# A decoder step on one core: new durations for the clocks that place small products, a search over priorities in the list scheduler, and a shorter patience in two passes

## The chip, the core and the metric

The kernel runs on one core of a Trainium2 chip. A core has five engines that each work through their own instructions in order: TensorE (PE in the profile, with its weight loads as PEld), VectorE (DVE), ScalarE (ACT), GpSimd (POOL) and SyncE (SP), which mostly issues DMA transfers. The metric is the device time of one execution in microseconds; the median of the runs counts.

## The reference

One layer of a hybrid decoder for 1024 prompt rows and 8 x 8 sample rows (1088 columns in all, features on the partitions): a normalised and modulated input, one projection to 34 blocks of 128 columns, a recurrent branch, a pooling branch, a gated merge, and an MLP.

```python
h = rms_norm(x, lp["norm_mix"]) * (1 + sc) + sh
P = h @ lp["w_in"]
pr, pp, pg = jnp.split(P, [RWKV_COLS, RWKV_COLS + POOL_WIDTH], axis=-1)
o_r, s_shift, s_wkv, v_first = rwkv7_branch(pr, shift0[l], wkv0[l], v_first, lp)
o_p, s_pool = pool_branch(pp, pool0[l], pos0, lp)
g_r, g_p = jnp.split(jax.nn.sigmoid(pg), 2, axis=-1)
merged = g_r * (o_r @ lp["w_br_rwkv"]) + g_p * (o_p @ lp["w_br_pool"])
x = x + gt * (merged @ lp["w_out"])
...
x = x + gt * (jnp.square(jax.nn.relu(h @ lp["w_ff1"])) @ lp["w_ff2"])

def step(S, inp):                                   # the recurrence, per head of 64
    r_t, w_t, k_t, v_t, kk_t, a_t = inp
    sa = jnp.einsum("bhvk,bhk->bhv", S, -kk_t)
    S = (S * w_t[:, :, None, :] + sa[..., None] * (kk_t * a_t)[:, :, None, :]
         + v_t[..., None] * k_t[:, :, None, :])
    return S, jnp.einsum("bhvk,bhk->bhv", S, r_t)
```

## The kernel before, in words

**Two kinds of products.** The large matrices run as *weight products*: a 128x128 piece of a weight, split by ScalarE into a rounded half `whi` and by VectorE into the rest `wlo` (read from `wraw`), times up to 364 columns of the split input (`hx`). They go into the PSUM banks `mm` (four) and are evicted to `px`, `d` or `t`. The recurrence runs beside them as *small products* in four *passes* f = 0 to 3 of two heads each, in the banks `w` (two) and `wc` (two). The recurrence is done in 16 chunks of 64 rows with a matrix inverse for each, and then a *chain* over the chunks.

**A pass, by the names in the profile.** `front` and `unit` make decays and scores (`w<-ra,bk`, `w<-kct,ra`, `w<-kct,bk`, `w<-uv,at`); `bonus` and `post` make sums over a head with a matrix of ones (`w<-wt,bones`). `inverse` runs on VectorE: fifteen pairs of a multiply and a reduction (`hv`, `tt`), then transposes (`iv`). `level` completes it with four groups of 32x32 products: `w<-hv,hv`, `w<-iv,hv`, `w<-hv,ao`, `w<-z,hv`. `affine` follows with `w<-at,z` and `wc<-ab,at` or `w<-ab,at`. `chain` takes the products `wc<-uv,ab` and `wc<-ab,uv`, then 16 steps in which the small products `wc<-S,ra` and `wc<-ra,S` use the state S that VectorE made in the step before. `sample` does the eight short sequences (`w<-uv,ak`, `w<-hv,ra` and others). `post(f - 1)` normalises and gates the output of the pass before (`w<-wt,sw` is its gate; in `post(3)` the sums are `w<-wt,kct`) and writes it to scratch in HBM (`d_or`); pass 0 has modulation products in that place (`wc<-wt,sT`, "ada"). The last weight products of this stage are the eight `op_job`s, whose evictions `px<-px,mm` and `d<-d,mm` are on VectorE; the next stage starts with `or_job(0)`, which needs the output of `post(3)` in its fourth quarter.

**What sets the order.** Python generators emit the kernel. `Pace.run` emits weight products one after the other and asks, between them, whether a small product may go: it may when `Clocks` holds its operands ready (`Need.at`, with a spare of 300 ns) at the present time of the emitted stream. If the last product was a full 128x128 one, the small one waits up to `wait` ns more for another that changes the shape of the array (its *patience*). Each instruction on another engine gets a duration in `Clocks.op` and a place on its engine in `Clocks.place`; each small product gets one in `K.took`. So these durations set the order on PE.

The same instructions are recorded in `Ledger`, with a second set of durations in `Ledger.cost` and `Ledger.product`. After the stage is emitted, `Ledger.schedule` *plays* it: a list scheduler in which PE keeps its order and the other engines take, of the instructions that are ready, the one with the least key. The key was the place in which it was emitted. `Ledger.fix` then pins the order of VectorE, and of SP from its 61st issue, to that of the play; ScalarE and GpSimd are not pinned.

## Time and profile before

| | |
|---|---|
| median of 3 runs | 1584.08 us (1583.99 to 1584.94) |
| the profiled execution | 1583.99 us |
| its span, first to last instruction | 1582.2 us |
| mean granted clock of TensorE | 0.994 |
| PE, PEld, DVE, ACT, POOL busy | 96%, 91%, 70%, 42%, 9% of the span |
| instructions | 34017 |

The stage with the small products lies from about 62 us (the first stage's end) to about 735 us. How to read the rows: a line is "engine line operation output<-inputs, shape, count", then the busy time, the mean duration, and the idle time just before with the one that ended it. In a timeline a row starts with its start and its length in us, and the bracket at its end is the engine's idle time before it, with what ended it. A row of the waits has the total, the number of waits and the longest. Nearly everything on VectorE and ScalarE has one line of the code, that of the recording helper, so the names of the tiles tell the groups apart. A plain fp32 product is recorded twice, which is why its counts are double those of the program.

### The profile page before, as it was taken

To read this page: it belongs to the slowest core of one execution; us is meant where nothing else is said; L and a number is where in the kernel's file an instruction comes from. 1 tells how busy PE (TensorE), PEld (TensorE's weight loads), DVE (VectorE), ACT (ScalarE), POOL (GpSimd) and SP (SyncE) were. 2 spreads that over 40 slices of the span, in tenths; PEclk is the share of its full clock that TensorE was granted. 3 is DMA by queue.
4 is the path that set the end of the run, shared out by engine and by line. 5 is a ranking of instruction groups with operands and counts; after the bars stand their busy time and mean duration, and the time that the engine had idled before them with its cause. 6 is when DMAs were issued, how large, how long until landed. Compare 5 with 4: busy or idle time off the path is not lost.

```text
span 1582.2 us, 34017 instructions
## 1 busy us (share of the span) xinstructions
PE 1526.2 (96%) x13777; PEld 1432.5 (91%) x13777; DVE 1111.3 (70%) x1944; ACT 658.5 (42%) x1285; POOL 147.9 (9%) x234
## 2 busy tenths in 40 slices
PE   4999999999999999999999999999999999999997
PEld 2998888898898899888899999999999999999997
DVE  5576668776777758556544797898767796666776
ACT  5454354355236433423222572222334344334652
POOL 3100100000000000112501210000000050000000
PEclk9999999999999999999999999999999999999999
DMA  9142523244324344854875555665436995664754
GB/s 367 63 136 83 182 86 110 93 133 149 111 78 150 116 125 139 305 188 169 310 280 181 185 196 186 221 219 191 146 146 223 396 348 199 211 208 148 231 164 159
DMA packets 136493, 290.04 MB, mean 183 GB/s; under 512 B 36976, under 2 KB 41072, under 8 KB 136336
## 3 DMA queue, kind: packets, MB, share of 16 engines
q1 hardware_dynamic: 129952, 266.75, 49.2%
q10 hardware_dynamic: 4320, 14.00, 2.6%
q0 software_dynamic: 2064, 7.13, 1.4%
q8 instruction: 108, 1.77, 0.5%
q14 instruction: 49, 0.40, 0.1%
HBM read 210.54 MB, written 77.28 MB: 182 GB/s over the span
## 4 chain that ended last, share of the span: by engine, by line
PE 48%; DVE 11%; DMA 7%; issue 2%; ACT 1%; SPq 0%; POOL 0%; DVEq 0%; ACTq 0%; POOLq 0%
PE mm L573 32%; PE wc L573 8%; PE w L573 7%; DVE hx L393 4%; DMA hid<-in_w_ff 2%; DVE wt L393 2%; DMA d_t<-hx 1%; DVE wlo L393 1%; DMA mg<-in_w_ff 1%; DMA wt<-d_bv 1%; DMA hid<-in_w_ada_mlp 1%; DVE hid L393 1%; DVE mg L393 1%; DVE sw L393 0%; DMA wraw<-in_w_br 0%
## 5 line engine op out<-in xcount | busy, mean ns | idle before, releaser
L573 PE MATMUL mm<-hx,whi 128*128 128x362 f32 (+2 forms) x2944 | 687.5, 321 | 8.4 <-DVE hx L393 2.4
L573 PEld LDWEIGHTS mm<-hx,whi 128*128 128x128 f32 x2944 | 494.7, 189 | 31.0 <-issue 9.4
L573 PE MATMUL mm<-hx,wlo 128*128 128x362 f32 (+2 forms) x1472 | 461.9, 314 | 1.2 <-DVE wlo L393 1.1
L573 PEld LDWEIGHTS mm<-hx,wlo 128*128 128x128 f32 x1472 | 278.1, 189 | 2.0 <-DVE wlo L393 2.0
L573 PE MATMUL mm<-mg,whi 128*128 128x272 f32 (+2 forms) x1312 | 249.0, 289 | 1.3 <-DVE t L393 0.8
L573 PEld LDWEIGHTS mm<-mg,whi 128*128 128x128 f32 x1312 | 205.3, 188 | 6.7 <-issue 2.7
L573 PE MATMUL mm<-mg,wlo 128*128 128x272 f32 (+2 forms) x656 | 188.5, 287 | 0.0
L573 PE MATMUL wc<-hx,whi 128*128 128x272 f32 x896 | 170.4, 287 | 0.0
L393 ACT ACTIVATE whi<-hid 128x512 fp32r<-128x512 f32 x128 | 80.4, 630 | 144.3 <-PE mm L573 53.3
L573 PEld LDWEIGHTS wc<-hx,whi 128*128 128x128 f32 x896 | 140.3, 188 | 0.0
L573 PE MATMUL wc<-hx,wlo 128*128 128x272 f32 x448 | 128.9, 288 | 0.7 <-DVE wlo L393 0.7
L573 PEld LDWEIGHTS mm<-mg,wlo 128*128 128x128 f32 x656 | 123.5, 188 | 0.0
L393 DVE TENSOR_TENSOR wlo<-hid,whi 128x512 fp32r<-128x512 f32 x128 | 88.0, 690 | 40.1 <-ACT whi L393 39.0
L393 DVE TENSOR_TENSOR wlo<-wraw,whi 128x512 fp32r<-128x512 f32 x82 | 58.3, 711 | 62.8 <-ACT whi L393 62.7
L573 PE MATMUL w<-hx,whi 128*128 128x272 f32 (+1 forms) x480 | 97.4, 296 | 1.6 <-ACT hx L393 1.5
L393 ACT ACTIVATE whi<-wraw 128x512 fp32r<-128x512 f32 x100 | 62.6, 627 | 67.2 <-PE mm L573 26.2
L393 POOL TENSOR_TENSOR hx<-hx,rs 128x64 f32<-128x64 f32 x24 | 36.8, 1532 | 568.9 <-DMA mg<-in_w_ff 374.9
L573 PEld LDWEIGHTS wc<-hx,wlo 128*128 128x128 f32 x448 | 84.2, 188 | 1.1 <-DVE wlo L393 1.1
L573 PEld LDWEIGHTS w<-hx,whi 128*128 128x128 f32 x480 | 77.0, 188 | 3.0 <-ACT hx L393 1.8
L573 PEld LDWEIGHTS mm<-mg,hx 128*128 128x128 f32 x576 | 72.8, 188 | 5.0 <-issue 5.0
L573 PE MATMUL mm<-mg,hx 128*128 128x272 f32 (+2 forms) x576 | 74.7, 289 | 0.0
L393 ACT ACTIVATE px<-mm 128x362 f32<-128x362 f32 (+3 forms) x113 | 46.4, 435 | 60.6 <-PE mm L573 57.3
(293 smaller groups left out, 2317.0 us busy)
## 6 DMA issues: line engine op xcount, KB each, us to landing
t<-d_t SPq DMA_DIRECT2D x56, 544.0 KB, 5.2
hid<-in_w_ff SPq DMA_DIRECT2D x110, 256.0 KB, 4.3
d_t<-hx SPq DMA_DIRECT2D x102, 272.0 KB, 2.6
hid<-in_w_ff SPq DMA_DIRECT2D x42, 512.0 KB, 3.8
wraw<-in_w_in SPq DMA_DIRECT2D x68, 256.0 KB, 2.8
mg<-in_w_ff SPq DMA_DIRECT2D x58, 256.0 KB, 5.3
hid<-in_w_ada_mlp SPq DMA_DIRECT2D x24, 512.0 KB, 6.1
d_th<-px SPq DMA_DIRECT2D x22, 544.0 KB, 3.0
```

Source lines behind the costliest of these rows:

```text
L393: r = f(*a, **kw)
L573: r = self.nc.tensor.matmul(out, lhsT, rhs, **kw)
```

## The change

1. `Clocks.op` takes an instruction's duration from `Ledger.cost` instead of its own rules, and `K.took` takes a small product's from `Ledger.product`.
2. `Ledger.schedule` is given the keys and returns, beside the orders, PE's idle time in the play and the PE instructions that waited over 150 ns. The new `Ledger.search` starts from the emitted places, with 150 taken off for each VectorE and ScalarE instruction that touches a tile `mm`, `S`, `wlo` or `whi`. It then takes 200 off the keys of what stands ahead of the six longest waits, plays again, and goes on while PE's idle time in the play falls, 40 times at most.
3. The patience, 1000 ns where nothing else was given, becomes 300 in passes 2 and 3.

```diff
 class Clocks.op
-            m = max([n] + [math.prod(x.shape[1:]) for x in ins])
-            if eng == "scalar":
-                ns = 160 + 0.9 * n
...
-            elif "reduce" in name:
-                ns = 90 + 1.25 * m
-            else:
-                ns = 150 + (0.8 if name == "tensor_scalar" else 1.05 if n > 100 else 1.6) * n
+            ns = self.ledger.cost(eng, name, out, ins, a)
+            tab = self.TABLE.get(a[2], 0) if name == "activation" else 0
+            if tab and tab != self.table:
+                ns, self.table = ns + 1283, tab
 class Ledger
-    def schedule(self):
+    def schedule(self, key):
...
-            heapq.heappush(queue[ops[i][0]], (ready[i], i))
+            heapq.heappush(queue[ops[i][0]], (ready[i], key[i], i))
...
+                idle = t - free[e] - extra
+                if idle > 1:
+                    lost += idle
+                    if idle > 150:
+                        late.append((idle, i))
...
-        return order
+        return lost, late, order, begun, ended, ready
+
+    def search(self, rounds=40):
+        ops = self.ops
+        n = len(ops)
+        names = [set(x.split("_")[0] for x in o[4]) for o in ops]
+        key = [i - (150 if o[0] in ("vector", "scalar") and ("mm" in w or "S" in w or "wlo" in w or "whi" in w) else 0) for i, (o, w) in enumerate(zip(ops, names))]
+        best = self.schedule(key)
+        for _ in range(rounds):
+            lost, late, order, begun, ended, ready = best
+            trial = list(key)
+            for idle, i in sorted(late, reverse=True)[:6]:
+                todo, seen = [i], set()
+                while todo and len(seen) < 12:
+                    j = todo.pop()
+                    if j in seen:
+                        continue
+                    seen.add(j)
+                    trial[j] -= 200
+                    todo += [k for k in ops[j][3] if ended[k] > begun[j] - 400 and ops[k][0] != "tensor"]
+            got = self.schedule(trial)
+            if got[0] >= lost:
+                break
+            best, key = got, trial
+        return best[2]
 
     def fix(self, tc):
-        order = self.schedule()
+        order = self.search()
 class K
     def took(self, n, mode):
         if not self.clocks.on:
             return max(n / 0.6 * min(mode) / 128, 30) + 3
-        if mode == (64, 128):
-            return n + 10
-        if mode == (64, 64):
-            return 170 if n < 16 else 2 * n if n > 256 else 40 + n / 2
-        return 20 if mode == (32, 32) else n / 0.6 + 5 if min(mode) > 32 else n / 1.2
+        return self.clocks.ledger.product(mode, n, F32)
...
-    def need(self, *aps, banks=("w",), wait=1000, spare=300, slack=0):
+    def need(self, *aps, banks=("w",), wait=None, spare=300, slack=0):
+        wait = self.patience if wait is None else wait
...
         for f in range(4):
+            self.patience = (1000,1000,300,300)[f]
```

No instruction is added or taken away on PE, VectorE, GpSimd or SP; on ScalarE 17 loads of activation tables are left of 19. What moves is shown at three places.

On PE in pass 0, between the second and the third group of 32x32 products (`iv` and `hv` are the halves of the inverse, `hv,ao` the next level, `wt,sT` the modulation products; the rows `mm` are weight products). Before:

```order
L573 MATMUL w_1976<-iv_1844,hv_1953 32x32 x64
L573 MATMUL wc_1749<-wt_1884,sT 32x512 x2
L573 MATMUL wc_1749<-wt_1886,sT 32x512 x2
L573 MATMUL w_2055<-hv_2041,ao_1185 32x32 x32
L573 MATMUL mm_1810<-hx_217,whi_1788 128x362
```

And now:

```order
L591 MATMUL w_2030<-iv_1862,hv_1983 32x32 x64
L591 MATMUL mm_2018<-hx_207,whi_1873 128x364
L591 MATMUL mm_2018<-hx_208,whi_1873 128x364
L591 MATMUL mm_2018<-hx_207,wlo_1874 128x364
L591 MATMUL mm_2019<-hx_207,whi_1873 128x362
L591 MATMUL mm_2019<-hx_208,whi_1873 128x362
L591 MATMUL mm_2019<-hx_207,wlo_1874 128x362
L591 MATMUL mm_2020<-hx_207,whi_1873 128x362
L591 MATMUL mm_2020<-hx_208,whi_1873 128x362
L591 MATMUL mm_2020<-hx_207,wlo_1874 128x362
L591 MATMUL wc_1757<-wt_1989,sT 32x512 x2
L591 MATMUL wc_1757<-wt_1991,sT 32x512 x2
```

The group `hv,ao` follows directly behind the last of these rows; nine weight products have moved in ahead of it.

On VectorE in pass 3, at the evictions of `op_job(0)` (`px<-px,mm`), the reciprocals and multiplies of `post(2)` (`wt`) and the transposes of the inverse (`iv`, `hv`). Before:

```order
L393 STREAM_TRANSPOSE iv_7288<-iv_7285 128x16x32 x2
L393 RECIPROCAL wt_7151<-wt_7151 128x182 x3
L393 RECIPROCAL wt_7151<-wt_7151 128x180
L393 RECIPROCAL wt_7151<-wt_7151 128x182
L393 RECIPROCAL wt_7151<-wt_7151 128x180
L393 TENSOR_TENSOR hv_7453<-w_7388,kct 128x512
L393 TENSOR_TENSOR wt_7149<-wt_7149,wt_7151 128x364
L393 TENSOR_TENSOR wt_7149<-wt_7149,wt_7151 128x362 x2
L393 STREAM_TRANSPOSE hv_7547<-w_7482 128x512
L393 TENSOR_TENSOR wt_7149<-wt_7149,wt_7556 128x1088
L393 SCALAR_TENSOR_TENSOR px_7380<-px_7380,mm_7382 128x364
```

And now:

```order
L411 STREAM_TRANSPOSE hv_7334<-iv_7330 128x16x32
L411 SCALAR_TENSOR_TENSOR px_7318<-px_7318,mm_7320 128x364
L411 SCALAR_TENSOR_TENSOR px_7318<-px_7318,mm_7321 128x362
L411 STREAM_TRANSPOSE iv_7333<-iv_7330 128x16x32
L411 TENSOR_TENSOR hv_7458<-w_7393,kct 128x512
L411 SCALAR_TENSOR_TENSOR px_7318<-px_7318,mm_7322 128x362
L411 TENSOR_TENSOR wlo_7466<-wraw_7463,whi_7465 128x512
L411 STREAM_TRANSPOSE iv_7333<-iv_7330 128x16x32
L411 TENSOR_TENSOR wt_7225<-wt_7223,wt_7224 128x362
L411 STREAM_TRANSPOSE hv_7552<-w_7487 128x512
L411 RECIPROCAL wt_7223<-wt_7223 128x182 x3
```

The evictions have moved ahead of the reciprocals and of the multiply by the loaded bonus (`wt_7556` before), and between the transposes.

On SP, at the load of pass 2's output for `post(2)` (`wt<-d_y`) and the loads of the pooling operands (`hx<-d_oph`, `hx<-d_opl`), which go into buffers that the last weight products of the projection free. Before:

```order
L393 DMA wt_7149<-d_y_72 128x1088
L393 DMA wraw_7265<-in_w_br 128x512
L393 DMA d_bv_69<-wt_7108 128x1088
L393 DMA d_th_104<-px_7001 128x1088
L393 DMA hx_7356<-d_oph_82 128x1088
```

And now:

```order
L411 DMA wraw_7284<-in_w_br 128x512
L411 DMA hx_7294<-d_oph_82 128x1088
L411 DMA hx_7296<-d_opl_86 128x1088
L411 DMA hx_7298<-d_oph_83 128x1088
L411 DMA hx_7300<-d_opl_87 128x1088
L411 DMA wt_7221<-d_y_72 128x1088
L411 DMA hx_7302<-d_oph_84 128x1088
```

The load of `d_y` has moved behind four loads of pooling operands.

## The prediction

> **What bounds the kernel now.** I read the page first: the span and the engines' busy shares.

> ```profile
> span 1582.2 us, 34017 instructions
> PE 1526.2 (96%) x13777; PEld 1432.5 (91%) x13777; DVE 1111.3 (70%) x1944; ACT 658.5 (42%) x1285; POOL 147.9 (9%) x234
> ```

> TensorE (PE) is the bound nearly everywhere, and no other engine is near full. The change reorders one stage only, from the first head product to the last piece of head work, so next comes the busy time by stage; it also tells how dense VectorE (DVE) stands between the chains of passes 1, 2 and 3. The columns are the stretch in us, its length, the busy time of PE, PEld, DVE, ACT and POOL, the granted clock, the DMA share and GB/s.

> ```profile
> 62.00:735.00 673.00, 654.23 (x7027) 587.45 (x7026) 463.13 (x843) 301.98 (x636) 47.10 (x136) 0.99 0.41 135
> ...
> 370.00:525.00 155.00, 151.75 (x1653) 135.75 (x1649) 116.42 (x213) 70.14 (x152) 7.88 (x19) 1.00 0.38 119
> 525.00:674.00 149.00, 144.67 (x1643) 130.13 (x1644) 101.69 (x186) 61.62 (x136) 8.40 (x17) 0.98 0.50 170
> ```

> In the reordered stage PE is idle 673.00 - 654.23 = 18.8 us, at a granted clock of 0.99. The products are the same before and after, so a better order can win only that idle time, what of PE's waits hides under modelled matmul ends, and the cost of changing between array shapes. The waits of PE and of its weight loads (PEld) in this stretch:

> ```profile
> PE wc L573 <- DVE S L393: 2.3, 4, 1.2
> PE mm L573 <- DVE px L393: 2.2, 1, 2.2
> PE w L573 <- DVE wt L393: 2.2, 3, 1.5
> PE w L573 <- ACT iv L393: 1.8, 3, 0.9
> PE mm L573 <- ACT px L393: 1.7, 3, 0.7
> PE w L573 <- ACT hx L393: 1.5, 1, 1.5
> PE w L573 <- DVE hv L393: 1.3, 2, 0.8
> PE w L573 <- DVE d L393: 1.2, 2, 0.9
> PE w L573 <- ACT hv L393: 1.1, 1, 1.1
> PE w L573 <- issue: 1.1, 1, 1.1
> PE w L573 <- ACT wt L393: 1.0, 1, 1.0
> PE w L609 <- DVE at L393: 0.7, 1, 0.7
> ...
> PEld wc L573 <- DVE S L393: 7.3, 10, 1.4
> ...
> PEld w L573 <- DVE wt L393: 3.8, 4, 1.8
> ...
> PEld w L573 <- DVE hv L393: 3.4, 3, 1.7
> ...
> PEld mm L573 <- DVE px L393: 2.5, 1, 2.5
> ```

> The twelve PE rows give 18.1 us in 23 waits, 0.79 us each. No one wait is large: the stage loses by many short stalls where a small product stands too close behind the VectorE or ScalarE (ACT) work that feeds it. The weight loads' waits are longer than PE's for the same cause (hv 3.4 against 1.3), so the idle time understates the loss. [...]

> **The change part by part.** *Durations in the clocks.* The last multiply of the inverse, over 450 elements, has 150 + 1.05 x 450 = 0.62 us in the old clocks and in the new; the reduction behind it had 90 + 1.25 x 450 = 0.65 and now has 1.06.

> ```profile
> 177.93 0.96 DVE L393 TENSOR_TENSOR hv<-hv,tt 128x450 f32<-128x450 f32 x1
> 178.92 0.62 DVE L393 TENSOR_REDUCE tt<-hv 128x30 f32<-128x450 f32 x1
> ...
> 188.97 1.07 PE L573 MATMUL wc<-wt,sT 128*32 128x512 f32 x8
> 189.97 0.69 PE L573 MATMUL w<-hv,ao 32*32 32x32 f32 x30
> 191.77 0.72 PE L573 MATMUL w<-hv,ao 32*32 32x32 f32 x34 [1.11 <-issue]
> ```

> The trace has 0.96 + 0.62 = 1.58 us for the pair, the old clocks 1.27, the new 1.69: products behind the inverse were put too early and are now put later, with a little to spare. In pass 0 the 32x32 products hv,ao stood directly behind iv,hv and the ada products and lost 1.11 us; now 9 weight products stand between. Pass 1's z,hv stands 21 weight products behind hv,ao instead of 6, pass 2's iv,hv 24 behind hv,hv instead of 3. I take the rows hv (1.3 + 1.1) and issue (1.1) as gone: 3.5 us. The row at (0.7) stays: its products still stand one group behind the bank that they wait for.

> ```profile
> 628.68 0.59 PE L573 MATMUL w<-wt,bones 128*128 128x362 f32 x2 [1.48 <-DVE wt L393]
> 725.50 0.88 PE L573 MATMUL w<-wt,kct 128*128 128x362 f32 x2 [1.00 <-ACT wt L393]
> ```

> The third piece of post(2)'s first sums (628.68) stood 6 weight products behind the first two and now stands 15: 1.5 us of the row wt. The last sums of post(3) (725.50) stand 30 behind the sums they need instead of 15, which is 2.5 us more room; 1.0 us. The wait after it (ACT hx, 1.5) stays, since the same 27 products stand between.

> *Evictions, splits and state ahead.* Of what the play orders only VectorE and SP are pinned, so this acts on VectorE.

> ```profile
> 636.25 7.01 DVE L393 RECIPROCAL wt<-wt 128x182 f32<-128x182 f32 x6
> ...
> 645.77 1.43 DVE L393 TENSOR_TENSOR wt<-wt,wt 128x364 f32<-128x364 f32 x3 [1.97 <-ACT wt L393]
> ...
> 648.82 1.29 DVE L393 TENSOR_TENSOR wt<-wt,wt 128x1088 f32<-128x1088 f32 x1 [0.99 <-DMA wt<-d_bv]
> 650.02 1.41 DVE L393 SCALAR_TENSOR_TENSOR px<-px,mm 128x364 f32<-128x364 f32 x3
> ...
> 650.60 0.60 PE L573 MATMUL mm<-hx,whi 128*128 128x362 f32 x2 [2.23 <-DVE px L393]
> ```

> The evictions of op_job(0) stood behind six reciprocals and a multiply that waited for a load; PE had no mm bank for 2.23 us. Now they stand ahead of both: 2.2 us gone. Behind them the inverse's transposes now start later, and iv,hv waits for those; its 12 weight products are the cover. S loses its closest steps: in passes 1 to 3 a chain step stood four small products behind the one before, now 9 weight products more in passes 1 and 2, and the 16 products ab,at in pass 3; I take half of 2.3, 1.2 us. Sum of idle time gone: 3.5 + 1.5 + 1.0 + 2.2 + 1.2 = 9.4 us. For the part under modelled ends the same rows of the weight loads allow 0 to 9.0 us more (7.3 + 3.8 + 3.4 + 2.5 less 2.3 + 2.2 + 1.3 + 2.2); I take 2, near the low end, because a load's wait is mostly covered by the matmul that still streams.

> *Patience 300 in the last passes, and array shapes.* A small product no longer waits to share a shape change. Counted over the stage, the built order has 275 changes of array shape instead of 261.

> ```profile
> 710.49 0.32 PE L573 MATMUL mm<-hx,wlo 128*128 128x362 f32 x1
> 710.74 0.27 PE L573 MATMUL wc<-S,ra 64*64 64x64 f32 x2
> ...
> 711.02 0.60 PE L573 MATMUL mm<-hx,whi 128*128 128x364 f32 x2
> 711.46 0.33 PE L573 MATMUL mm<-hx,wlo 128*128 128x364 f32 x1
> ```

> Weight products start 0.165 us apart. From 710.49 to 711.46 stand three of them (0.50 us) and one chain step: 0.97 - 0.50 = 0.47 us for the step with two changes, of which 0.085 on the way in (0.25 - 0.165) and 0.11 on the way out (711.02 to 711.46 less 0.33). So a change costs 0.10 us, bounded by 0.085 and 0.11, and 14 cost 1.4 us. [...]

> *What is late next.* The new order has close places of its own: pass 2's at,z 6 weight products behind z,hv (21 before), pass 3's uv,ab 6 weight and two gate products behind at,z (15 weight products before), and a chain step of pass 3 that follows the last with 3 weight and one gate product between. Three at the mean 0.79 us: 2.4 us. On SP, post(2)'s load of y now stands behind four loads of op rows that wait for hx slots; landings of such loads near that place:

> ```profile
> wt<-d_y SPq DMA_DIRECT2D x1, 544.0 KB, 5.2
> ...
> wt<-d_x SPq DMA_DIRECT2D x1, 544.0 KB, 7.9
> wt<-d_bv SPq DMA_DIRECT2D x1, 544.0 KB, 11.6
> ```

> Between the product that frees the slots and the first sums of y stand 57 weight products, 9.4 us. The load needs its landing, about 1.1 us on SP and twice 0.48 us (1.43 / 3) to split: 7.3 us at 5.2 and no wait, 13.7 at 11.6 and 4.3 us. I take 2.1, the middle. Behind it on VectorE stand the last steps of pass 3's inverse, which is the same wait and not counted twice. The loss that comes back is bounded by 0 and by all 11.4; I take 2.4 + 2.1 = 4.5 us. The two ACT_TABLE_LOADs that fall away lie on an engine 42% busy: 0.

> Sum: -9.4 - 2 + 1.4 + 4.5 = -5.5 us. The profiled execution took 1583.99 us (its span 1582.2 and 1.8 around it), 0.09 under the median 1584.08: 1583.99 - 5.5 = 1578.5, which I predict.

> **The rivals.** *It does little.* ScalarE is ordered in the play but not pinned in the program, and the rows iv, px and hx of ACT (5.0 us) show waits that no place cures. If only what VectorE's own rows show comes off, the gain is 2.2 + 1.2 - 1.4 = 2.0 us: 1582, and 1585.4 with nothing but the shape changes. For it: the waits are short and many, so one removed lets PE reach the next sooner. Against it: the spacings named grow by 1.5 us or more each.

> *Slower: VectorE becomes the bound between the last two chains.* Pass 2's chain starts 96 weight products later than before and pass 3's at the same place, so the work of 525 to 674 us gets 96 x 0.165 = 15.8 us less: 101.69 us in 133.2, 76.3%, where it now runs at 68.2% and the densest stretch (370 to 525) at 75.1%. If the queue holds 75.1% the stretch is 2.2 us longer, at 68.2% 15.9 us. It decides below 71.7% (141.9 us, 8.7 over), and gives 1578.5 + 8.7 to 1578.5 + 15.9, in the middle 1591. For it: one in-order queue with head-of-line waits at both densities. Against it: much of the idle time at 68.2% is VectorE waiting for PE, which closer work removes.

> **How the numbers follow.** Forecast 0.60 (1570 to 1581), little 0.25 (1581 to 1587), VectorE-bound 0.15 (1587 to 1594). This kernel's measurement tells about 0.2%, 3.2 us, from no change: below 1580.9 is faster, above 1587.2 slower. So faster 0.60, same 0.25, slower 0.15. The low end is the sum with no loss back and two thirds of the hidden waits gone: -9.4 - 6 + 1.4 = -14.0, 1570; the high end leaves out the third case and the worst of the second: 1586. That leaves under 0.2 outside.

> **What would show it.** Right: PE's idle time between 62 us and the end of head work near 12 to 15 us; no wait for DVE px over 1 us; the hv and issue rows gone; the stage ending 4 to 8 us earlier and everything after it unchanged in length. Wrong: a wait for DVE wt or DMA at post(2)'s first sums (the y load), VectorE above 75% busy with PE waiting between the last two chains, or shape changes dearer than 0.11 us. What would make it wrong above all is a stall I could not place, since every VectorE row has moved.

## The result, and the profile after

The changed kernel is slower: 1594.62 us median of 6 runs (1591.73 to 1595.67) against 1584.51 (1583.72 to 1586.35), ratio 1.0059 with a 95% interval of 1.0046 to 1.0072. On another chip, beside other runs, it was 1.0042 (1.0028 to 1.0056). The prediction was 1578.5 us, range 1570 to 1586. Its profiled execution took 1594.58 us; the first lines of its page:

```profile
span 1592.7 us, 34023 instructions
...
PE 1533.0 (96%) x13777; PEld 1437.9 (90%) x13777; DVE 1113.3 (70%) x1944; ACT 657.8 (41%) x1283; POOL 155.4 (10%) x234
```

The span grew by 10.5 us. At equal counts of weight products the two traces stand 1.3 us apart when the stage begins (weight product 100 starts at 60.9 us before and at 62.2 now; in two other runs of the changed order, after_again and y_ahead, at 61.8 and 60.7, so this is hardly the work of the change), 10.0 us apart when head work ends, and 10.4 us at the end. So the loss lies in the reordered stage. Its row (columns as in the prediction: stretch, length, busy PE, PEld, DVE, ACT, POOL, granted clock, DMA share, GB/s), two stretches of it, and the stretch from pass 2's chain to pass 3's, after and before:

```profile
62.00:746.00 684.00, 662.01 (x7042) 594.49 (x7041) 465.45 (x844) 301.11 (x634) 52.55 (x138) 0.99 0.41 134
380.00:535.00 155.00, 154.57 (x1773) 138.98 (x1773) 113.15 (x210) 66.99 (x147) 7.33 (x18) 1.00 0.33 106
535.00:684.00 149.00, 139.19 (x1694) 122.43 (x1692) 104.24 (x193) 67.11 (x146) 9.28 (x17) 0.98 0.50 169
...
546.20:681.96 135.76, 126.22 (x1510) 111.33 (x1509) 98.55 (x183) 60.41 (x133) 9.28 (x17) 0.98 0.52 175
```

```profile
527.29:675.80 148.51, 144.18 (x1640) 129.87 (x1638) 102.23 (x188) 62.02 (x135) 8.40 (x17) 0.98 0.51 175
```

PE is idle 684.00 - 662.01 = 22.0 us in the stage, 3.2 more than before. Nearly all of 380 to 535 us is full (0.4 us idle), but 535 to 684 us loses 9.8. The waits of PE in the stage:

```profile
PE w L591 <- DVE wt L411: 5.5, 3, 2.5
PE w L591 <- issue: 3.6, 1, 3.6
PE mm L591 <- ACT px L411: 3.1, 2, 1.9
PE w L591 <- DVE hv L411: 2.3, 1, 2.3
PE w L591 <- ACT uv L411: 2.0, 3, 1.4
PE w L591 <- ACT hx L411: 1.9, 1, 1.9
PE w L591 <- DVE ra L411: 1.2, 1, 1.2
```

Before, the stage lost by 24 waits of over 0.15 us, of which one was over 2 us; now there are 16, fewer and longer ones: three over 2 us, eight over 1.3. That matters for a second reason, the granted clock. In the traces of both kernels it has two values, 1.00 and 0.50, and all its changes lie a multiple of 3.41 us apart (after: 3.41, 17.07, 23.89, 58.03, 276.48 us and others; before: 6.83 and 610.99). The stretches below are such steps; the third number is PE's busy time, the last but two the clock. First after, at 352 and at 372 us, then before, at 650 us:

```profile
349.60:353.01 3.41, 1.52 (x9) 1.20 (x8) 1.72 (x3) 3.12 (x5) 2.44 (x4) 1.00 0.16 49
353.01:356.43 3.42, 3.42 (x9) 2.42 (x8) 0.00 (x0) 0.95 (x2) 0.00 (x0) 0.50 0.48 193
370.08:373.49 3.41, 1.45 (x10) 1.41 (x10) 1.89 (x3) 1.41 (x3) 0.11 (x1) 1.00 0.71 285
373.49:376.91 3.42, 3.42 (x14) 3.02 (x14) 0.16 (x1) 2.38 (x5) 0.54 (x1) 0.50 0.28 79
```

```profile
648.31:651.73 3.42, 1.19 (x8) 1.13 (x8) 2.91 (x5) 2.90 (x5) 1.02 (x2) 1.00 0.96 381
651.73:658.55 6.82, 6.82 (x79) 5.81 (x79) 0.31 (x1) 1.66 (x3) 0.63 (x2) 0.50 0.81 259
```

A step in which PE was busy for less than half of it (1.52, 1.45, 1.19 of 3.41 us) was followed by one at half clock, in which PE is "busy" all the time (3.42 of 3.42 us) and its weight products start 0.30 us apart instead of 0.165 (after, 373.7 to 376.4 us). I count half of such a step, 1.7 us, as lost, an estimate from the clock of 0.50; the spacing of the weight products would give 1.5. Over the 20 profiles, of the steps at full clock between 45 and 1500 us, all 24 that were under 0.4 busy were followed by half clock, 25 of 34 at 0.4 to 0.5, 15 of 54 at 0.5 to 0.6, and 5 of 8311 above. In the traces of the two kernels the emptiest of these steps was 0.31 busy (after, 649.97 us). The stage had one such stretch before (6.83 us), and five after (17.07 us, behind the waits at 352, 372, 653, 680 and 742 us): (17.07 - 6.83) / 2 = 5.1 us. The account of the profiled execution: 1.3 ahead of the stage, 3.2 idle time, 5.1 half clock, and 0.9 for the rest, against 1.4 forecast for changes of array shape.

Whether a wait was followed by half clock depended here also on where it fell among the steps, and that differed from run to run. The wait for px at 352 us is equally long, 1.89 or 1.90 us, in eight of the traces. In two of them it lay inside one step, which was 0.45 busy, and half clock followed. In the other six the edge of a step cut it, both steps stayed at 0.55 busy or more, and no half clock followed. Here is the wait in the changed kernel, and then the wait and both steps in after_thin (a run that is described below):

```profile
352.20 0.60 PE L591 MATMUL mm<-hx,whi 128*128 128x362 f32 x2 [1.89 <-ACT px L411]
```
```profile
350.99 0.60 PE L591 MATMUL mm<-hx,whi 128*128 128x362 f32 x2 [1.90 <-ACT px L411]
```

```profile
346.86:350.28 3.42, 2.23 (x14) 1.93 (x12) 3.18 (x5) 1.75 (x2) 3.18 (x4) 1.00 0.31 57
350.28:353.69 3.41, 2.70 (x13) 2.24 (x14) 0.00 (x0) 2.32 (x6) 0.62 (x2) 1.00 0.56 219
```

So the 5.1 us is in part the luck of this execution; the runs of after_again, below, lose 2.8 us by the clock on average.

### The profile page after: what moved, and what is told of

It is laid out like the page before. It is cut to its first block, busy times and chain, and to the rows that moved or that the text cites. A ratio compares the mean times of both kernels' runs of the same rounds, so it can differ in the third digit from the quotient of the medians.

```text
span 1592.7 us, 34023 instructions
## 1 busy us (share of the span) xinstructions
PE 1533.0 (96%) x13777; PEld 1437.9 (90%) x13777; DVE 1113.3 (70%) x1944; ACT 657.8 (41%) x1283; POOL 155.4 (10%) x234
## 4 chain that ended last, share of the span: by engine, by line
PE 75%; DVE 11%; DMA 7%; ACT 3%; issue 2%; SPq 1%; POOL 0%; ACTq 0%; DVEq 0%; POOLq 0%
PE mm L591 50%; PE w L591 13%; PE wc L591 11%; DVE hx L411 3%; DVE wt L411 1%; DMA d_t<-hx 1%; DMA wt<-d_x 1%; DVE wlo L411 1%; ACT wt L411 1%; DMA hid<-in_w_ada_mlp 1%; DVE hv L411 1%; SPq L411 1%; DMA hid<-in_w_ff 1%; DMA wt<-d_y 1%; DMA x<-in_xT 1%
## 5 line engine op out<-in xcount | busy, mean ns | idle before, releaser
L411 DVE TENSOR_TENSOR wlo<-wraw,whi 128x512 fp32r<-128x512 f32 x82 | 58.5, 714 | 72.6 <-ACT whi L411 72.3
L411 POOL TENSOR_TENSOR hx<-hx,rs 128x64 f32<-128x64 f32 x24 | 40.5, 1686 | 564.9 <-DVE rs L411 542.9
## 6 DMA issues: line engine op xcount, KB each, us to landing
t<-d_t SPq DMA_DIRECT2D x56, 544.0 KB, 5.4
d_th<-px SPq DMA_DIRECT2D x22, 544.0 KB, 3.0
```

What stands on the lines that cost most here:

```text
L411: r = f(*a, **kw)
```

## The experiments

Each row: the ratio to the kernel before on the same chip, and the mean us over it, split by each run's mean granted clock c: half of its time at half clock is (1 - c) times its time, as the two traces show no clock but 1.00 and 0.50 (c has three digits, so a mean is good to about 0.5 us), the rest is everything else.

| kernel | ratio, 95% | mean us over before | of it half clock | rest |
|---|---|---|---|---|
| search_alone | 1.0011 (1.0000 to 1.0022) | 1.9 | 2.1 | -0.2 |
| patience_alone | 1.0110 (1.0091 to 1.0130) | 17.2 | 10.1 | 7.2 |
| clocks_alone | 1.0186 (1.0162 to 1.0211) | 28.7 | 19.4 | 9.3 |
| no_clocks (patience, search) | 1.0068 (1.0047 to 1.0090) | 10.9 | 5.8 | 5.1 |
| no_patience (clocks, search) | 1.0170 (1.0141 to 1.0199) | 27.4 | 18.4 | 9.0 |
| no_search (clocks, patience) | 1.0071 (1.0056 to 1.0086) | 11.0 | 7.3 | 3.7 |
| after_again (all three) | 1.0042 (1.0028 to 1.0056) | 6.1 | 2.8 | 3.3 |
| after_thin | 0.9989 (0.9973 to 1.0006) | -1.6 | -2.0 | 0.3 |
| before_thin | 0.9983 (0.9963 to 1.0004) | -1.6 | 0.1 | -1.7 |
| y_ahead | 1.0045 (1.0031 to 1.0059) | 7.0 | 2.3 | 4.7 |
| after_fixed | 1.0016 (1.0000 to 1.0033) | 3.4 | 1.2 | 2.2 |
| thin_y | 0.9985 (0.9971 to 0.9998) | -2.2 | -1.2 | -1.0 |
| thin_fixed | 0.9991 (0.9977 to 1.0005) | -1.5 | -2.0 | 0.5 |
| after_filled | 1.0059 (1.0039 to 1.0080) | 9.4 | 1.2 | 8.2 |
| after_kept | 1.0035 (1.0017 to 1.0054) | 6.1 | -1.5 | 7.6 |
| before_filled | 1.0010 (0.9996 to 1.0025) | 2.3 | -0.5 | 2.9 |
| before_kept | 1.0009 (0.9991 to 1.0027) | 2.7 | -0.2 | 2.9 |
| before_px | 0.9960 (0.9946 to 0.9974) | -6.1 | -3.7 | -2.4 |

**The three parts, alone and in pairs.** A part that is off has its old code again: for the durations the old lines of Clocks.op and K.took, for the search and the patience these edits:

```
-    def search(self, rounds=40):
+    def search(self, rounds=0):
-        key = [i - (150 if ... else 0) for i, (o, w) in enumerate(zip(ops, names))]
+        key = list(range(n))
```
```
-            self.patience = (1000,1000,300,300)[f]
+            self.patience = (1000,1000,1000,1000)[f]
```

TensorE's order comes from durations and patience alone, the search moves only VectorE and SyncE.

> The kernel before with one part of the change alone: the clocks take the fitted durations (both in Clocks.op and in K.took); VectorE's play is unsearched and patience stays 1000 in all passes. Theory A (cover): the fitted durations put every small product later among the weight products; pass 3's chain, which began behind weight product 2556 of the stage in both kernels, begins in this build behind the last one, 2736, so that its twenty steps and the last products of head work run with nothing beside them. A step with nothing beside it takes about 1.4 us, so 20 to 45 us more than before: 1605 to 1630 us, most of it after 700 us, with the granted clock at half there. Theory B (each part moves the time a little, and the parts add): within 6 us of before, 1578 to 1590 us.

> The kernel before with patience 300 in passes 2 and 3 alone (old durations, unsearched play). Pass 3's chain begins behind weight product 2454, 102 earlier than before, and the load of y of pass 2 stands on SyncE ahead of the op rows. Theory A (what is late in the changed kernel is the y load and what VectorE queues behind it): no such stall here, so no loss: 1578 to 1587 us. Theory B (patience itself costs, by more changes of array shape and small products nearer to what feeds them): 1588 to 1595 us.

> The kernel before with the searched play alone (evictions, splits and state 150 places ahead, then up to 40 rounds; old durations, patience 1000). The order on TensorE is that of before, only VectorE and SyncE differ. Theory A: the one stall of before for a bank that VectorE had not emptied (2.2 us at 650 us) goes, and with it the 6.83 us at half clock behind it (3.4 us lost): 4 to 6 us less, 1578 to 1580.5 us. Theory B (VectorE's order matters only by its idle time at PE): 1.5 to 2.5 us less, 1582 to 1583 us. Theory C (the moved evictions make others late): 1586 us or more.

> The changed kernel without its search (fitted durations and patience 300 as in it, VectorE's play in plain order). TensorE's order is that of the changed kernel. Theory A (the loss is in TensorE's order and the late load of y, which stands behind four op rows here too): 1589 to 1598 us. Theory B (the moved evictions on VectorE make the loss): back to 1582 to 1586 us.

> The changed kernel with the old durations in its clocks (searched play and patience 300 in the last passes as in it). TensorE's order is that of the kernel before with patience 300 alone, which took 1600.8 us. Theory A (TensorE's order sets the time, VectorE's play moves it by 2 us): 1598 to 1604 us. Theory B (the searched play mends what patience spoils): 1584 to 1594 us.

> The changed kernel with patience 1000 in all passes (fitted durations and searched play as in it). Pass 3's chain begins behind the last weight product of the stage, 2736, as with the fitted durations alone, which took 1.0186 of before. Theory A (the cover of the last chain decides, VectorE's order does little): 1.014 to 1.020 of before, so that patience 300 is worth 13 to 24 us to the changed kernel. Theory B (the searched play makes up for the missing cover): 1.003 to 1.010.

The changed kernel once more, with no edit:

> The changed kernel once more, unaltered, on the chip of the three runs beside it, so that its time and its time at half clock stand beside theirs: 1.004 to 1.008 of before, with 1.5 to 3 stretches of 3.41 us at half clock more than before.

No part is a gain by itself. The durations alone cost 28.7 us: theory A, the last chain outside its cover (the trace is 11.7 us ahead of the kernel before at weight product 2730 and 28.6 behind at 2736, with the chain between them). With them and the search, the whole of that chain (from 712 to 762 us of no_patience) looks so:

```profile
712.00:762.00 50.00, 38.14 (x454) 27.46 (x453) 25.95 (x51) 14.63 (x33) 2.68 (x4) 0.73 0.22 74
```

PE idles 11.9 of 50 us there and the clock is 0.73. Patience 300 brings that chain back from weight product 2736 to 2556: 1.0170 against 1.0042 to 1.0059, 18 to 21 us. On the old durations, where nothing needed mending, it costs 17 us (theory B, and more than B gave). The largest wait there is of 5.9 us:

```profile
534.98 1.33 PE L605 MATMUL w<-ab,at 64*64 64x128 f32 x10 [5.87 <-ACT uv L425]
```
```profile
533.28 1.39 ACT L425 ACTIVATE wt<-wt,part 128x512 f32<-128x512 f32 x2 [6.04 <-DMA wt<-d_x]
534.57 0.36 ACT L425 ACTIVATE uv<-w 64x256 f32<-64x256 f32 x1
```

ScalarE, which the play orders but the program does not pin, stands 6.04 us before a load that the next pass needs, and the eviction uv<-w that PE waits for stands behind it. The search alone makes no measurable difference where I had expected 4 to 6 us less. Its three evictions of op_job(0) were not moved ahead of what blocks them: they still stand behind the multiply that waits for bv, and now behind a split too, and PE waits 4.0 instead of 2.2 us.

```profile
653.46 1.29 DVE L425 TENSOR_TENSOR wt<-wt,wt 128x1088 f32<-128x1088 f32 x1 [1.06 <-DMA wt<-d_bv]
655.87 0.69 DVE L425 TENSOR_TENSOR wlo<-wraw,whi 128x512 fp32r<-128x512 f32 x1 [1.12 <-ACT whi L425]
656.48 1.41 DVE L425 SCALAR_TENSOR_TENSOR px<-px,mm 128x364 f32<-128x364 f32 x3
```

Beside the other parts it was worth more. no_search came out as theory A has it: TensorE's order and the late load of y hold the loss. But PE waits there for px of VectorE at two places, 1.22 and 1.82 us, where the changed kernel has no such wait. no_clocks, at the edge of theory A's numbers, keeps the wait behind that ScalarE queue (5.76 us) and stands at 1.0068, against 1.0110 without the search.

**The wait inside a group of small products, 372 us.** PE had done 126 of the 128 products iv,hv of pass 1 and stood still before the last two, with nothing in the profile that it waited for. The core's DMA engines were full at that time; one of their packets was a 16 KB block of the kind "instruction". PE's rows and the queues from 366 to 372 us (packets, MB, share):

```profile
367.21 1.27 PE L591 MATMUL w<-iv,hv 32*32 32x32 f32 x126
372.04 0.22 PE L591 MATMUL w<-iv,hv 32*32 32x32 f32 x2 [3.56 <-issue]
```
```profile
q1 hardware_dynamic: 800, 2.33, 98.9%
q8 instruction: 1, 0.02, 1.0%
```

after_thin cuts the stores of pass 0's output (and those of the op rows of group 1 likewise) to 16 of 1088 columns, so it leaves out most of what they carry; GpSimd writes those rows earlier, from another tile:

```
-            nc.sync.dma_start(self.d_or[0][f], hi.bitcast(F32))
+            (self.thin if f == 0 else nc.sync.dma_start)(self.d_or[0][f], hi.bitcast(F32))
...
+    def thin(self, out, src):
...
+        r = nc.sync.real.dma_start(out[:, 0:16], src[:, 0:16])
```

> The changed kernel with four stores of 544 KB near 361 to 367 us (or rows of pass 0, op rows of group 1) cut to 16 of 1088 columns, so that the outputs are wrong; those rows are written earlier by GpSimd from another tile. Everything else stands in the same order. Theory A (TensorE's instructions come by the same DMA engines: two groups of 128 small products stand close together at 363 and 367 us, the DMA engines are full from 362 to 372 us, and TensorE stops inside the second group for 3.56 us until its next block of instructions lands): with half of that traffic gone the wait inside the group falls under 1.2 us and its stretch at half clock goes: 3 to 5 us less, 1589.5 to 1592 us. Theory B (the wait is the rate at which small products use up instructions, whatever the DMA does): the wait stays over 2.5 us, 1593 to 1596 us.

> The control to the thin stores: the kernel before with the same four stores cut to 16 columns (the outputs are wrong). In this kernel the groups of 128 small products of pass 1's inverse stand at 339 and 348 us, ahead of the stores at 354 to 364 us. Theory A (the stores hurt only where they meet such a group): no change, 0.999 to 1.001 of before, while the changed kernel gained 0.4 to 0.7% by them. Theory B (less traffic helps any order): 0.993 to 0.997.

```profile
364.34 1.27 PE L591 MATMUL w<-iv,hv 32*32 32x32 f32 x126
366.18 0.22 PE L591 MATMUL w<-iv,hv 32*32 32x32 f32 x2 [0.57 <-issue]
```
```profile
q1 hardware_dynamic: 582, 0.27, 19.0%
q8 instruction: 2, 0.03, 2.6%
```

The wait falls from 3.56 to 0.57 us, and the half clock behind it goes: between weight products 1400 and 1500 the trace gains 4.5 us. In no_search, with the same order on TensorE, it stood in the same group, for 4.64 us. So the stores' traffic makes this wait. That it acts through late instructions is what the traces fit: over the 20 profiles PE has 42 waits for "issue" of over 0.4 us in the stage, and every one of them ended 1.22 to 1.61 us after a 16 KB instruction packet of queue q8 had landed (1.41 us in the changed kernel, 1.61 in no_search). The packet itself took 0.97 us with the stores and 0.98 without, but it started 5.7 us behind the one before it, and 4.6 with the stores thinned. No run changed the fetch by itself. Over the runs after_thin stands 0.5 to 0.7% below the changed kernel, more than expected, and the control, before_thin, 0.17% below its own with an interval that holds 1; so the most of it, but perhaps not all, belongs to the changed order. The trace of after_thin cannot tell how much: it ends 9.4 us sooner than the changed kernel's, of which 4.5 us are this wait and 4.6 the half clock behind three waits that are as long in both traces (at 352, 680 and 742 us).

**SyncE's and VectorE's order, 640 to 655 us.** SyncE's rows of the changed kernel, what waited for the load of y on ScalarE and VectorE, and PE:

```profile
628.10 0.45 SPq L411 DMA_DIRECT2D hx<-d_oph  x1
...
630.92 0.65 SPq L411 DMA_DIRECT2D wt<-d_y  x1
```
```profile
640.28 1.30 ACT L411 ACTIVATE wt<-wt 128x364 fp32r<-128x364 f32 x3 [4.62 <-DMA wt<-d_y]
```
```profile
640.82 1.43 DVE L411 TENSOR_TENSOR wt<-wt,wt 128x364 fp32r<-128x364 f32 x3 [2.15 <-ACT wt L411]
```
```profile
647.55 0.60 PE L591 MATMUL w<-wt,bones 128*128 128x362 f32 x2 [2.53 <-DVE wt L411]
653.01 1.77 PE L591 MATMUL w<-hv,hv 32*32 32x32 f32 x128 [2.34 <-DVE hv L411]
```

y_ahead moves SyncE's last load of y of pass 2 ahead, to one weight tile behind the last store of that pass. after_fixed (the diff) puts it right behind that store and moves, on VectorE, iv<-tt and hv<-iv of pass 3's inverse to right behind the last reduction. thin_y and thin_fixed add the thin stores:

```
         order = self.search()
+        line = order["vector"]
...
+        order["vector"] = [i for i in line[:k + 1] if i not in move] + move + [i for i in line[k + 1:] if i not in move]
+        line = order["sync"]
...
+        line.insert(j + 1, line.pop(k))
```

> The changed kernel with one transfer moved: SyncE issues the load of y of pass 2 right behind the next weight tile after its second half was stored, ahead of a store of px, a weight tile and four op rows. Nothing else changes in the stage. Theory A (the late y load makes the waits at 647 us, and by VectorE's splits and reciprocals behind it those at 653 and 680 us): the load lands near 626 instead of 640 us, those three waits (2.5, 2.3 and 1.4 us) and two stretches at half clock (1.7 us each) go: 6 to 10 us less, 1585 to 1589 us. Theory B (VectorE's order behind it sets those waits): 1592 to 1596 us.

> The changed kernel with two things moved: SyncE issues the load of y of pass 2 right behind the stores of y, and VectorE's iv<-tt and the transpose behind it (pass 3's inverse) stand right behind the last reduction, ahead of the splits and squares of y. Theory A (queue order at these places sets the waits at 647 and 653 us): both fall under 1 us (2.5 and 2.3 before) with the half clock behind them: 4 to 6 us less than the changed kernel, 1.000 to 1.003 of before. Theory B (mending one wait shows the next): the wait moves on to the products behind it, 1.003 to 1.006.

> The changed kernel with both: the four stores near 361 to 367 us cut to 16 columns (the outputs are wrong), and the load of y of pass 2 issued right behind the stores of y. Theory A (two separate waits that add): 2 to 4 us less than with the thin stores alone, 0.9965 to 0.998 of before. Theory B (the y load is hidden anyway): 0.9985 to 0.9995 as with the thin stores alone.

> The changed kernel with both causes taken away: the four stores near 361 to 367 us cut to 16 columns (the outputs are wrong), the load of y of pass 2 issued right behind the stores of y, and pass 3's iv<-tt and the transpose behind it ahead of y's splits on VectorE. Theory A (the two causes are the loss, and the rest of the change is a gain): 2.5 to 5 us less than with the thin stores alone, 0.9955 to 0.998 of before. Theory B (the next wait takes their place): 0.998 to 1.000.

The load alone took the 2.53 us away and not the 2.34 (2.38 there), and the ratio moved by no more than its interval: theory A was right on one wait of three. With the inverse's two instructions moved as well, both fall under 1 us, but a wait for issue of 2.5 us comes behind them:

```profile
PE w L600 <- issue: 2.5, 1, 2.5
...
PE w L600 <- DVE hv L420: 0.9, 2, 0.7
...
PE w L600 <- DVE wt L420: 0.3, 1, 0.3
```

after_fixed reaches 1.0016, within theory A's numbers, but its trace does not show that the move on VectorE did it. Between weight products 2400 and 2600 it gains 2.8 us on the changed kernel, and y_ahead without that move gains 3.0. In after_again, which has no edit, the wait for hv is 0.94 us too, with a wait for issue of 1.44 behind it. So the late load of y is shown as the cause of its own wait, and the cause of the wait behind it stays open. The two causes do not add over the runs: with the thin stores and one or both of the moves the kernel stands at 0.9985 and 0.9991, as with the thin stores alone (0.9989), theory B. In the traces the moves are worth 0.9 us there, from after_thin to thin_fixed: the wait for y goes (2.53 to 0.27 us), and those for hv, issue and z behind it grow from 2.7 to 3.8 us together. With both taken away the change is level with the kernel before (0.9983 with the same stores thinned); a gain of the size that I forecast is not there.

**What the half clock costs by itself.** Extra products fill a wait, so that PE is busy while it waits (the edit of after_kept; the other kernels differ in the places and in the factor):

```
         self.mm(ps, w[0], xl, start=False, stop=False, **kw)
+        self.n3 = getattr(self, "n3", 0) + 1
+        for _ in range({457: 2, 473: 3, 822: 2, 827: 2, 851: 1}.get(self.n3, 0)):
+            self.nc.tensor.matmul(ps, self.zero, xl.bitcast(F32), start=False, stop=False)
```

> The changed kernel with 13 extra products that add zeros to an open mm bank (zeros times hx in fp32, 128x128 by 362, about 0.65 us each): two ahead of each of the five waits at 352, 647, 653, 680 and 742 us and three ahead of the one at 372 us; the outputs stay the same and the order of everything else in the stage too. Theory A (clock): the waits last as long, but TensorE is busy in them, so that no window of 3.41 us falls under half busy and the five stretches at half clock in the stage go; each cost 1.7 us, so up to 8.5 us less than the changed kernel: 1586 to 1590 us. Theory B (the loss is the idle time and the order; the clock follows it and costs little): the extra 8.4 us of products lie in idle time at best: 1594 to 1600 us.

> The kernel before with two extra products that add zeros to the open third bank of op_job(0), ahead of the 2.2 us wait at 650 us (1.3 us of fp32 products in the place of idle time). Theory A (the clock follows how busy TensorE is): the wait ends when it did, TensorE is idle in it for about 0.9 us instead of 2.2, the stretch at half clock behind it goes, and with it up to 3.4 us; by the trace the products behind it start 1.7 to 3.4 us sooner. Theory B (the clock has another cause, such as the transfers at that place): the half clock stays, no change or up to 1 us more.

> The kernel before with two extra products by a tile of zeros (128x128, never written again) into the open third bank of op_job(0), ahead of the wait of 2.2 us at 650 us; they are 1.3 us of fp32 products. Theory A (the clock follows how busy TensorE was in the 3.41 us before): the wait for px ends when it did (the products behind it start at the same time), TensorE is idle for 0.9 us instead of 2.2 and no half clock follows: the products from there on come 1.7 to 3.4 us sooner, 0.998 to 0.999 of before. Theory B (only the idle time counts): the same time as before, 0.9995 to 1.0005.

> The changed kernel with extra products by a tile of zeros into an open mm bank: two ahead of the waits at 352, 647 and 653 us, three ahead of the one at 372 us, one ahead of the one at 680 us (6.5 us of products in all). Theory A (clock): the waits end when they did and two to three stretches of 3.41 us at half clock fewer: 3.5 to 5 us less than the changed kernel, 1.0015 to 1.003 of before. Theory B (idle time and order only): 1.004 to 1.008.

In the two "filled" kernels the factor was the tile z, which I had taken for zeros: it holds the inverse's blocks, ScalarE writes it, and the filling products waited for that (2.5 us in before_filled). They tell nothing. With true zeros, before_kept is clean at the place: PE busy 1.97 of 3.42 us, no half clock behind it, and its products come 2.5 us sooner between weight products 2400 and 2600, of which 0.8 is less idle time (1.45 instead of 2.23 us; the whole wait could not be filled).

```profile
648.58:652.00 3.42, 1.97 (x9) 1.18 (x8) 2.28 (x4) 3.01 (x6) 0.38 (x1) 1.00 0.95 377
652.00:655.40 3.40, 3.40 (x78) 3.12 (x77) 0.94 (x2) 0.93 (x2) 0.73 (x2) 1.00 0.79 184
```

But it did not get faster. In its trace the 2.1 us that it was ahead at the end of head work are lost at 776 us, where the next stage waits for a load, longer than before (0.85 us) and long enough for 6.83 us at half clock:

```profile
776.39 1.05 PE L573 MATMUL wc<-hid,sT 128*32 128x512 f32 x4 [2.92 <-DMA hid<-in_w_ada_mlp]
```

after_kept has the time at half clock of a kernel without the change (-1.5), 4.3 us less than after_again, and pays for 6.5 us of products with 4.3 us of the rest: the time at half clock fell where PE was kept busy, but filling is no gain. This is theory A's mechanism and only part of its time.

**One wait removed in the kernel before.** VectorE's three evictions px<-px,mm of op_job(0) go to right ahead of the multiply that waits for bv.

```
         order = self.schedule()
+        line = order["vector"]
...
+        move = [i for i in line[k:] if self.io[i][0].endswith("_7380")][:3]
...
+        order["vector"] = line[:k] + move + [i for i in line[k:] if i not in move]
```

> The kernel before with three instructions of VectorE moved: the evictions of op_job(0) (px<-px,mm, at 650.02 us) stand ahead of the multiply that waits for the load of bv (648.82 us). Nothing else changes. Theory A (a wait costs its idle time and, if it empties half of a 3.41 us window, 1.7 us for each window at half clock behind it): the 2.2 us wait shrinks to under 0.5 us and the 6.83 us at half clock go: 3.5 to 5.5 us less than before in that place, 0.9965 to 0.9985 of before over the runs. Theory B (a wait costs its idle time alone): 1.5 to 2 us less, 0.9987 to 0.9995. If it is the faster one it is also a version that beats both kernels.

```profile
650.41 1.38 DVE L399 SCALAR_TENSOR_TENSOR px<-px,mm 128x364 f32<-128x364 f32 x3
651.97 1.29 DVE L399 TENSOR_TENSOR wt<-wt,wt 128x1088 f32<-128x1088 f32 x1 [0.19 <-DMA wt<-d_bv]
```
```profile
651.00:655.00 4.00, 4.00 (x81) 3.73 (x81) 2.77 (x4) 3.90 (x7) 1.11 (x2) 1.00 1.03 412
```

The wait for px and the half clock are gone; between weight products 2400 and 2600 the trace gains 5.3 us, 1.9 of idle time and 3.4 of clock, as theory A has it. The runs give 0.9960 (0.9946 to 0.9974), a little better than theory A's 0.9965 to 0.9985: three instructions moved ahead of one are worth 6 us, and this version beats both kernels.

## Why the prediction was wrong, point by point

- **The named waits: right, and too small.** S (2.3 us on PE, 7.3 on PEld) left no row on PE and 0.8 us on PEld; px of VectorE (2.2) is gone, which took the search beside the other parts (no_search has two such waits, search_alone a longer one); so are ACT wt (1.0) and the places of hv that I named. The wait behind the last sums stayed (1.9). The row at (0.7), which I had staying, went too. Taken product by product, 21 of the 24 waits are gone, 14.5 us where I had 9.4.
- **What is late next: wrong, and the main step.** I bounded it by 11.4 us and took 4.5. The trace has 17.6: 13 products that did not wait before hold 16.2 us, and the three waits that stayed grew by 1.4. Eight of the new ones are over 1 us: issue 3.56, hv 2.34, ACT px 1.89, wt 1.64 at 318 us, uv 1.36, wt 1.35 at 92 us, ACT px 1.23 at 590 us, ra 1.20. PE's idle time was to fall from 18.8 to 13.9 us and rose to 22.0. None of the three close places that I named shows a wait.
- **The y load: right in kind and size** (2.1 taken, 2.53 measured, at sums that had waited 1.48 before). But I called the inverse behind it the same wait; it was a second one, 2.34 us, which stayed when the load came sooner (y_ahead, 2.38). Its own cause stays open: it fell to 0.7 us with VectorE's two instructions moved and to 0.94 in after_again with no edit.
- **The issue row: misread.** I took the 1.1 us before hv,ao as a product too close behind VectorE and wrote it off as gone. It ended 1.44 us after an instruction packet had landed, so it is of the kind that became 3.56 us when the later order brought pass 1's groups of 128 products into the stores at 361 to 367 us. I followed what each moved product waits for, and not what it moves into.
- **The half clock: left out.** No term of the sum had it, though the row of 525 to 674 us that I quoted shows the clock at 0.98. It has 5.1 us of the loss. It would also have given the px wait its price in that trace, 5.3 us with the clock (before_px) and not 2.2.
- **Hidden 2 us: not seen.** With it and 1.4 for the array shapes (275 changes in the trace against 261) the rest of the account would be 0.6 us less than before; it is 0.9 more. No run parts the two, and none shows the 2 us: the four rows of weight loads that they came from stood 9.0 us above PE's before (17.0 against 8.0) and 3.7 now (11.5 against 7.8), and the rest did not fall with them.
- **The rival "VectorE becomes the bound" gave 1587 to 1594.** The stretch between the last two chains took 135.76 us where 133.2 were forecast, 2.6 longer, with VectorE at 98.55 / 135.76 = 72.6%, above the 71.7% at which it was to decide. So it did not decide, and the time of the rival was met by other means.

Together: 8.1 us more idle time than forecast, 5.1 of clock, 2 that did not come and 1.3 ahead of the stage, less 0.5 at the array shapes, make 16.0, against 1594.6 - 1578.5 = 16.1. The two largest, the waits and the clock, are the error; the start and some of the clock are luck of this execution.

## What to carry to other kernels

Price a wait by its length and by the clock step behind it: here one that emptied half of a 3.41 us step cost by my estimate 1.7 us more for each step at half clock, so one wait of 2.2 us cost 5.3 (before_px), and one of 1.9 us cost nothing more where the edge of a step cut it. Here, removing one long wait (before_px) gained 6 us and shortening many gained none. When an order is moved, check each moved group of small products against the transfers that it will then stand among, and each in-order queue for an instruction that waits for a load ahead of an eviction. Try the parts of such a change alone and in pairs: here none gained alone, one lost 28.7 us, and another was needed only to mend that.
